# Hybrid attention and recurrence step: two gate chunks exchanged, modulation sums placed a chunk later, streams interleaved by other stage lengths

## Chip, cores and metric

One core of one Trainium2 chip. The metric is the device time of one execution in microseconds, smaller is better; the kernel before takes 966.97 us, the median of three runs (965.69 to 968.09).

## What is computed

Two layers (DEPTH = 2) over 640 tokens of 1,024 numbers: 512 latent tokens and 128 context tokens, all in float32. In each layer the tokens are modulated, go through one wide input projection, feed three parallel head groups, and come back through one output projection, a gate and a layer norm.

```python
shift, scale, gate = modulation(cond, w_ada[l], b_ada[l])      # cond differs for latent and context
h = x * (1.0 + scale) + shift
parts = split(h @ w_in[l])
# A: grouped-query attention, 8 query heads on 2 key heads, rms-normed and rotated q, k
# B: differential attention, 4 heads, two softmax maps each: p0 - lam * p1, rms-normed
# C: gated linear recurrence, 4 heads, forward and backward, state (64 x 64) per head
y = concat(A * silu(a_g), B * silu(d_g), C * silu(r_g)) @ w_out[l]
x = layer_norm(ALPHA * x + gate * y)
```

Latent tokens attend to 128 cached tokens besides their own 512, and their recurrence starts from a cached state; context tokens see themselves alone, and their keys, values and final states are outputs too.

## The kernel before, in words

**Tiles.** All 640 tokens are kept at once: SBUF buffers of 128 x 640 ("gran", 49 of them), 8 for the modulated input's high part and 8 for its low part. Every projection is three products, high x high, high x low, low x high (lines 351 to 353 for chunks with tokens on the partitions, 372 to 374 for transposed ones). The input projection is cut into 14 chunks of 256 columns (CHUNKS): 0 is q and k of the first head pair of B, 1 its values, 2 the values of C, 3 and 4 the two *gate chunks of the first recurrence pair*: 3 holds that pair's query gate (SiLU) and forward decay, 4 its backward decay and output gate (SiLU). 5 to 13 are the rest. A chunk's weights are loaded by SP (line 241) into a pool of three, cast by ScalarE (261) and their remainder taken by VectorE (262).

**Two kinds of work.** The chunks form the background: `bg_stream` (in `layer`) goes through them in the order of ORDER[l], with modulation products between them where MODS[l] says so. The foreground is six streams written as generators: `prep_stream` (rotation, lines 423 to 426; high and low parts, lines 99 to 103; transposes, line 1079), `sp_stream` (first pass of scores: product 1001 or 1005, row maximum on VectorE 1008, exponential on ScalarE 1009; then per pair of items the corrections, `finish_m` 983 to 986, turned into query rows by 1017 and 1020; for context tokens 1033, 1036, 1040, 1045, 1047), `pv_stream` (second scores 1057 to 1060, exponential 1066, values 1124), `hgrn_stream` (the recurrence, lines 822 to 978; its levels are line 882), and two that norm and gate the results.

**What sets the order.** `drive` writes all streams' code out in one order: it keeps a clock of its own, takes the first stream of PRIO[l] that is due, and otherwise the background. Each `yield` of a stage says how much TensorE time it takes and how long until the stream's next stage is due; these pairs are the table COST[l]. So COST sets only the order in which code is written. A scheduler of the framework then lays the instructions out for each engine, from that order; every engine runs its own list strictly in order, and SP's list of transfers too. LOOK, SPA, KG, OUTQ and PB are further constants that don't change here.

**Modulation sums.** `mod_next` multiplies 256 columns of the modulation weights (line 280) and ScalarE copies the result (`ms`, line 283). The sums over it (`mod_out`: two transposes on TensorE, 292; a reduction and an addition on VectorE, 295 and 299) wait in a list until `flush` is called. `bg_stream` calls it at the PEND-th piece of the next chunk and at every chunk's end:

```python
for r in chunks[i]() if kind == "w" else mod_next(l if i >= 8 else l + 1, i):
    n += kind == "w"
    if n == PEND:
        flush()
    ...
flush() if kind == "w" else None
```

**SiLU and decay.** `silu_block` reads a product out of PSUM by ScalarE (384), runs two more ScalarE steps (385, 386) and multiplies with the product, still in PSUM, on VectorE (387). `decay_block` takes its product out of PSUM in one VectorE clamp (565) and does all else in SBUF. The chunks' products use two PSUM banks ("A"), so a product waits until the one before the last has left its bank; everything small shares three banks ("B").

Of the kernel before, what the change touches and what calls it, by code (L numbers as in the profile page):

```python
# [37 lines left out]
WB = 6  # L38
KK = 8
LOOK = (0, 1)  # L40
PEND = 2
SPA = (2, 3)
KG = 4
OUTQ = (3, 2, 0, 1)
PB = dict(A=2, B=3, O=1)
OTAG = "O"
CTAG = "B"
COST = (dict(mod=(0.43, 2.59), norm0=(0.0, 4.0), norm1=(0.4, 0.96), gmix=(0.28, 21.63), h_exp=(0.06, 2.01),
              h_diag=(2.13, 0.37), h_lvl=(0.0, 3.0), h_mm=(0.99, 0.0), h_kst=(0.0, 1.4), h_tr=(0.0, 0.0),
              h_u=(7.96, 1.11), h_out=(22.66, 1.86), s_max=(0.0, 1.59), s_tr=(0.0, 0.4), c_max=(0.44, 3.0),  # L50
              c_tr=(1.29, 0.0), d_rq=(0.0, 1.96), d_rk=(0.53, 1.34), d_spl=(0.77, 1.38), d_tr=(4.22, 0.0),
              d_ctx=(0.72, 1.8), pv_c=(0.0, 0.0), g_ss=(0.0, 1.28), g_rope=(0.0, 2.5), g_k=(0.0, 0.71),
              g_ctx=(0.0, 1.2), g_spl=(0.0, 0.87), g_tr=(1.22, 2.24), pv_c2=(4.13, 5.2), s_g=(0.49, 1.79),
              s_d=(0.38, 1.88), pv_e=(0.77, 0.7), pv_g=(1.3, 0.56), pv_d=(1.04, 0.21)),
        dict(mod=(1.04, 9.27), norm0=(0.36, 5.04), norm1=(0.0, 0.68), gmix=(0.28, 21.63), h_exp=(0.0, 1.81),
              h_diag=(1.81, 1.27), h_lvl=(0.0, 3.0), h_mm=(0.89, 0.0), h_kst=(0.0, 1.63), h_tr=(0.0, 0.0),
              h_u=(7.96, 1.11), h_out=(22.66, 1.86), s_max=(0.0, 1.59), s_tr=(0.0, 0.19), c_max=(0.36, 3.68),
              c_tr=(1.29, 0.0), d_rq=(0.0, 1.96), d_rk=(0.53, 1.34), d_spl=(0.72, 1.39), d_tr=(3.82, 0.0),
              d_ctx=(0.6, 1.8), pv_c=(0.0, 0.28), g_ss=(0.0, 1.28), g_rope=(1.04, 4.49), g_k=(0.0, 0.71),
              g_ctx=(0.0, 1.2), g_spl=(0.07, 0.35), g_tr=(1.22, 2.24), pv_c2=(4.13, 5.4), s_g=(0.43, 1.82),  # L60
              s_d=(0.37, 1.67), pv_e=(0.77, 0.97), pv_g=(1.3, 0.73), pv_d=(0.86, 1.01)))
PRIO = ((1, 0, 2, 3, 5, 4),
        (0, 5, 1, 2, 3, 4))
ORDER = ((0, 1, 3, 4, 2, 5, 6, 8, 7, 9, 10, 11, 12, 13),
         (0, 1, 3, 2, 4, 5, 7, 6, 8, 9, 10, 11, 12, 13))
MODS = ({1: (8,), 2: (9,), 3: (10,), 4: (11,), 5: (0,), 6: (1,), 7: (2,), 8: (3,), 9: (4,), 10: (5,), 12: (6,), 13: (7,)},
        {0: (8,), 3: (9,), 9: (10,), 10: (11,)})
# [7 lines left out]
def hybrid_kernel(ctx: ExitStack, tc: tile.TileContext, A, cst, outs):  # L75
# [425 lines left out]
    def layer(l, hT, first, defer):  # L501
        cost.update(COST[l])
        lam_init = LAM0[l]
# [199 lines left out]
        def bg_stream():  # L703
            for kind, i in steps(l):
                n = 0
# [4 lines that stand above are left out]
# [703 lines left out]
```

## Time and profile before

| what | value |
|---|---|
| device time, median of 3 runs | 966.97 us (965.69 to 968.09) |
| the profiled execution | 973.31 us, span of its instructions 971.5 us |
| TensorE (PE) busy | 911.6 us, 94% of the span |
| weight loads on TensorE (PEld) | 751.6 us, 77% |
| VectorE (DVE) busy | 596.6 us, 61% |
| ScalarE (ACT) busy | 583.7 us, 60% |
| GpSimd (POOL) busy | 78.6 us, 8% |
| granted TensorE clock, mean | 0.977 of full speed |
| DMA | 100.36 MB, 103 GB/s over the span |
| chain that ended last | PE 65%, DVE 10%, DMA 10%, ACT 10%, issue 3%, SP's queue 2% |

A busy share is an average over stages. Where TensorE is busy nearly all the time, the lines to look for are its idle times and what ended each of them, and the stretches in which its clock was not granted in full. Matmuls overlap, so their listed durations are longer than the distance from one start to the next.

### The profile page before, as it was taken

What the parts mean: (1) busy time and instruction counts of PE and PEld (TensorE: products, weight loads), DVE (VectorE), ACT (ScalarE), POOL (GpSimd) and SP (SyncE); (2) the same over time, 40 slices, a digit from 0 to 9 for tenths busy, and PEclk for the clock granted to TensorE, in tenths of its full rate; (3) what the DMA queues carried; (4) which work ended last, traced back from release to release, by engine and by line L of the source; (5) the groups of instructions that cost most, each with busy time, mean ns of one, the idle gap of its engine ahead of it and who ended that gap; (6) DMA issues with size and microseconds to landing.
All of it is one profiled execution on the core that took longest, in us unless ns stands there. A gap on an engine that the chain in (4) does not pass through costs nothing.

```text
span 971.5 us, 20546 instructions
## 1 busy us (share of the span) xinstructions
PE 911.6 (94%) x8197; PEld 751.6 (77%) x8197; DVE 596.6 (61%) x1344; ACT 583.7 (60%) x1309; POOL 78.6 (8%) x113
## 2 busy tenths in 40 slices
PE   6999899999999989999999999999989998999995
PEld 3698776887878748687989997878768875878895
DVE  2346555945868875343698455685585885543467
ACT  2334665567667768773265468656766785886311
POOL 1000000200000100110023000020000000110012
PEclk9999897999999999999999999999989999999998
DMA  9856520344442121225624453025124121212322
GB/s 295 282 152 167 153 74 27 105 121 119 125 117 55 44 75 44 58 79 179 175 81 132 134 144 106 2 62 125 50 76 111 50 74 31 72 42 71 128 98 98
DMA packets 103583, 100.36 MB, mean 103 GB/s; under 512 B 9416, under 2 KB 91840, under 8 KB 103488
## 3 DMA queue, kind: packets, MB, share of 16 engines
q1 hardware_dynamic: 103488, 99.05, 34.7%
q8 instruction: 65, 1.06, 0.5%
q14 instruction: 30, 0.25, 0.1%
HBM read 77.25 MB, written 6.31 MB: 86 GB/s over the span
## 4 chain that ended last, share of the span: by engine, by line
PE 65%; DVE 10%; DMA 10%; ACT 10%; issue 3%; SPq 2%; DVEq 0%; POOL 0%; ACTq 0%; POOLq 0%
PE pO L1124 8%; PE pA L351 8%; PE pA L353 8%; PE pA L352 7%; PE pS L1001 5%; PE pA L374 4%; PE pA L372 4%; PE pA L373 4%; DMA wraw<-in_w_in_dram 3%; DMA wa<-in_w_ada_dram 2%; PE pB L1060 2%; PE pB L1057 2%; PE pS L1005 2%; ACT pS L1009 2%; PE pB L280 2%
## 5 line engine op out<-in xcount | busy, mean ns | idle before, releaser
L1008 DVE TENSOR_REDUCE nmx<-pS 128x1 f32<-128x640 f32 x128 | 105.4, 823 | 120.2 <-PE pS L1001 71.4
L351 PE MATMUL pA<-wh,mh 128*128 128x256 f32 x600 | 171.3, 286 | 1.6 <-DVE gate_t L387 1.3
L353 PE MATMUL pA<-wh,ml 128*128 128x256 f32 x600 | 170.8, 285 | 0.2 <-DVE ml L535 0.2
L352 PE MATMUL pA<-wl,mh 128*128 128x256 f32 x600 | 170.0, 284 | 0.0
L261 ACT CAST wh<-wraw 128x512 fp32r<-128x512 f32 x144 | 86.4, 621 | 75.5 <-PE pA L353 28.5
L262 DVE TENSOR_TENSOR wl<-wraw,wh 128x512 fp32r<-128x512 f32 x144 | 96.5, 695 | 53.1 <-ACT wh L261 50.0
L1009 ACT ACTIVATE pS<-pS,nmx 128x640 f32<-128x640 f32 x128 | 98.2, 767 | 50.4 <-DVE nmx L1008 48.2
L351 PEld LDWEIGHTS pA<-wh,mh 128*128 128x128 f32 x600 | 114.9, 191 | 4.2 <-DVE gate_t L387 1.6
L353 PEld LDWEIGHTS pA<-wh,ml 128*128 128x128 f32 x600 | 114.7, 191 | 1.6 <-issue 0.7
L352 PEld LDWEIGHTS pA<-wl,mh 128*128 128x128 f32 x600 | 114.7, 191 | 0.8 <-issue 0.6
L1066 ACT ACTIVATE PT<-pB 128x512 f32<-128x512 f32 x160 | 89.9, 599 | 28.8 <-PE pB L1060 15.6
L351 PE MATMUL pA<-wh,hh 128*128 128x256 f32 x240 | 71.4, 298 | 1.3 <-DVE gate_t L387 1.3
L372 PE MATMUL pA<-hh,wh 128*128 128x320 f32 x224 | 70.8, 316 | 0.0
L353 PE MATMUL pA<-wh,hl 128*128 128x256 f32 x240 | 70.7, 295 | 0.0
L352 PE MATMUL pA<-wl,hh 128*128 128x256 f32 x240 | 70.2, 293 | 0.0
L372 PE MATMUL pA<-mh,wh 128*128 128x320 f32 x224 | 70.2, 313 | 0.0
L374 PE MATMUL pA<-mh,wl 128*128 128x320 f32 x224 | 69.9, 312 | 0.0
L374 PE MATMUL pA<-hh,wl 128*128 128x320 f32 x224 | 69.7, 311 | 0.0
L373 PE MATMUL pA<-ml,wh 128*128 128x320 f32 x224 | 69.6, 311 | 0.0
L373 PE MATMUL pA<-hl,wh 128*128 128x320 f32 x224 | 69.5, 310 | 0.0
L1124 PE MATMUL pO<-PT,tk 128*64 128x512 f32 x256 | 67.0, 631 | 0.2 <-ACT PT L1066 0.2
L351 PEld LDWEIGHTS pA<-wh,hh 128*128 128x128 f32 x240 | 48.0, 200 | 3.8 <-DVE gate_t L387 1.6
(285 smaller groups left out, 1944.1 us busy)
## 6 DMA issues: line engine op xcount, KB each, us to landing
wraw<-in_w_in_dram SPq DMA_DIRECT2D x32, 512.0 KB
wraw<-in_w_ada_dram SPq DMA_DIRECT2D x32, 512.0 KB
wraw<-in_w_in_dram SPq DMA_DIRECT2D x48, 256.0 KB
wa<-in_w_ada_dram SPq DMA_DIRECT2D x32, 256.0 KB
wraw<-in_w_out_dram SPq DMA_DIRECT2D x16, 512.0 KB
Q<-Q SPq DMA_DIRECT2D x32, 160.0 KB
KD<-dkh SPq DMA_DIRECT2D x32, 96.0 KB
QD<-dqh SPq DMA_DIRECT2D x32, 80.0 KB
```

Of the source, the lines that this page charges most:

```text
L261: nc.scalar.copy(hi[n], src)
L262: tt(out=lo[n], in0=src, in1=hi[n].bitcast(F32), op=ALU.subtract)
L351: mm(out=ps[:, o:o + 256], lhsT=hi[k][:, sl], rhs=a, start=(n == 0), stop=False)
L352: mm(out=ps[:, o:o + 256], lhsT=hi[k][:, sl], rhs=b, start=False, stop=False)
L353: mm(out=ps[:, o:o + 256], lhsT=lo[k][:, sl], rhs=a, start=False, stop=(n == last))
L372: mm(out=ps, lhsT=wa, rhs=hi[k][:, sl], start=(k == 0), stop=False)
L373: mm(out=ps, lhsT=wa, rhs=lo[k][:, sl], start=False, stop=False)
L374: mm(out=ps, lhsT=wb, rhs=hi[k][:, sl], start=False, stop=(k == KB - 1))
L1008: dve.tensor_reduce(out=nmx[:, t, i:i + 1], in_=sv, axis=AX.XY, op=ALU.max, negate=True)
L1009: act(sv, sv, AF.Exp, bias=nmx[:, t, i:i + 1], accum_out=den[:, t, i:i + 1])
L1066: return pt, act(pt, ps, AF.Exp).ins
L1124: x = mm(out=o[64 * (i % 2):64 * (i % 2) + 64], lhsT=value(k, i % 2), rhs=pt, start=k == 0, stop=k == 4)
```

## The change

Four things, all of them constants that set the order in which the same instructions stand: ORDER[0] takes chunk 4 before chunk 3; PEND goes from 2 to 0, so that the list of modulation sums is no longer emptied inside a chunk but at its end; and both tables of COST get other values for some stages. PRIO has the same values on one line, so every line behind it is one lower in the changed file (262 becomes 261, and so on). The diff, without the unchanged lines of COST:

```diff
-PEND = 2
+PEND = 0
...
-COST = (dict(mod=(0.43, 2.59), norm0=(0.0, 4.0), norm1=(0.4, 0.96), gmix=(0.28, 21.63), h_exp=(0.06, 2.01),
+COST = (dict(mod=(0.43, 2.59), norm0=(0.0, 4.0), norm1=(0.4, 0.96), gmix=(0.35, 21.63), h_exp=(0.06, 2.01),
...
-              h_u=(7.96, 1.11), h_out=(22.66, 1.86), s_max=(0.0, 1.59), s_tr=(0.0, 0.4), c_max=(0.44, 3.0),
-              c_tr=(1.29, 0.0), d_rq=(0.0, 1.96), d_rk=(0.53, 1.34), d_spl=(0.77, 1.38), d_tr=(4.22, 0.0),
-              d_ctx=(0.72, 1.8), pv_c=(0.0, 0.0), g_ss=(0.0, 1.28), g_rope=(0.0, 2.5), g_k=(0.0, 0.71),
+              h_u=(7.96, 1.11), h_out=(22.66, 1.86), s_max=(0.0, 1.59), s_tr=(0.0, 0.2), c_max=(0.44, 3.0),
+              c_tr=(1.29, 0.0), d_rq=(0.0, 1.96), d_rk=(0.53, 1.34), d_spl=(0.77, 1.91), d_tr=(4.22, 0.0),
+              d_ctx=(0.72, 1.8), pv_c=(0.3, 0.3), g_ss=(0.0, 1.28), g_rope=(0.0, 2.5), g_k=(0.0, 0.71),
...
-        dict(mod=(1.04, 9.27), norm0=(0.36, 5.04), norm1=(0.0, 0.68), gmix=(0.28, 21.63), h_exp=(0.0, 1.81),
-              h_diag=(1.81, 1.27), h_lvl=(0.0, 3.0), h_mm=(0.89, 0.0), h_kst=(0.0, 1.63), h_tr=(0.0, 0.0),
-              h_u=(7.96, 1.11), h_out=(22.66, 1.86), s_max=(0.0, 1.59), s_tr=(0.0, 0.19), c_max=(0.36, 3.68),
-              c_tr=(1.29, 0.0), d_rq=(0.0, 1.96), d_rk=(0.53, 1.34), d_spl=(0.72, 1.39), d_tr=(3.82, 0.0),
+        dict(mod=(1.04, 9.27), norm0=(0.36, 5.34), norm1=(0.0, 0.68), gmix=(0.15, 21.63), h_exp=(0.0, 1.75),
+              h_diag=(1.09, 1.27), h_lvl=(0.0, 3.0), h_mm=(0.89, 0.0), h_kst=(0.0, 1.63), h_tr=(0.0, 0.0),
+              h_u=(7.96, 1.11), h_out=(22.66, 2.33), s_max=(0.3, 1.59), s_tr=(0.0, 0.19), c_max=(0.36, 3.68),
+              c_tr=(1.29, 0.0), d_rq=(0.0, 1.96), d_rk=(0.53, 1.34), d_spl=(0.72, 1.39), d_tr=(2.29, 0.0),
...
-              g_ctx=(0.0, 1.2), g_spl=(0.07, 0.35), g_tr=(1.22, 2.24), pv_c2=(4.13, 5.4), s_g=(0.43, 1.82),
-              s_d=(0.37, 1.67), pv_e=(0.77, 0.97), pv_g=(1.3, 0.73), pv_d=(0.86, 1.01)))
+              g_ctx=(0.0, 1.2), g_spl=(0.07, 0.35), g_tr=(1.22, 2.24), pv_c2=(4.13, 5.4), s_g=(0.34, 2.27),
+              s_d=(0.37, 1.67), pv_e=(0.77, 0.97), pv_g=(1.3, 0.44), pv_d=(0.86, 1.01)))
...
-ORDER = ((0, 1, 3, 4, 2, 5, 6, 8, 7, 9, 10, 11, 12, 13),
+ORDER = ((0, 1, 4, 3, 2, 5, 6, 8, 7, 9, 10, 11, 12, 13),
```

What this does to the engines' lists, at three places. The names: tk is a token chunk's result (here keys or queries being rotated), he the decay, gate_t a SiLU's result, sm and mod the modulation sums, dql and dkl low halves of queries and keys, wl the low half of a weight, mhl and mhc the corrections of scores (latent, context), QD and KD query and key rows of B, PT exponentials, dcv cached values.

**Place 1**, VectorE, first gate chunk of layer 0, the kernel before:

```order
L295 TENSOR_REDUCE sm<-pB 128x4
L299 SCALAR_TENSOR_TENSOR mod_105<-sm,vv 128x4
L387 TENSOR_TENSOR gate_t<-pA,sge 128x320
L423 TENSOR_TENSOR rope<-tk,cs 128x16x8 x4
L425 TENSOR_TENSOR tk<-tk,cs 128x512
L103 SCALAR_TENSOR_TENSOR dql<-pB,dqh 128x512
L262 TENSOR_TENSOR wl<-wraw,wh 128x512 x2
L426 TENSOR_TENSOR tk<-tk,rope 128x512
L387 TENSOR_TENSOR gate_t<-pA,sge 128x320
L100 TENSOR_TENSOR dkl<-pB,dkh 128x512
L100 TENSOR_TENSOR dkl<-pB,dkh 128x256
L103 SCALAR_TENSOR_TENSOR dql<-pB,dqh 128x128
```

VectorE in the change, the same place:

```order
L564 TENSOR_SCALAR he<-pA 128x320
L422 TENSOR_TENSOR rope<-tk,cs 128x16x8 x4
L424 TENSOR_TENSOR tk<-tk,cs 128x512
L425 TENSOR_TENSOR tk<-tk,rope 128x512
L102 SCALAR_TENSOR_TENSOR dql<-pB,dqh 128x512
L99 TENSOR_TENSOR dkl<-pB,dkh 128x512
L261 TENSOR_TENSOR wl<-wraw,wh 128x512 x2
L99 TENSOR_TENSOR dkl<-pB,dkh 128x256
L564 TENSOR_SCALAR he<-pA 128x320
L102 SCALAR_TENSOR_TENSOR dql<-pB,dqh 128x128
```

The modulation sums are gone from here, the clamp he stands where the SiLU's multiply stood, and the last rotation step (426, now 425) stands ahead of the weight's wl and not behind it.

**Place 2**, ScalarE at the end of a chunk that ends in a SiLU, with the copy ms of a modulation product (in the kernel before the second gate chunk, followed by the token chunk of C's values):

```order
L574 ACTIVATE hs<-hs,lbs 128x640
L283 COPY ms<-pB 128x256
L384 ACTIVATE sge<-pA 128x320
L1009 ACTIVATE pS,den<-pS,nmx 128x2x320
L385 ACTIVATE sge<-sge,cc 128x320
L386 ACTIVATE sge<-sge 128x320
```

ScalarE in the change (the first gate chunk, followed by the second):

```order
L573 ACTIVATE hs<-hs,lbs 128x640
L383 ACTIVATE sge<-pA 128x320
L282 COPY ms<-pB 128x256
L384 ACTIVATE sge<-sge,cc 128x320
L385 ACTIVATE sge<-sge 128x320
```

The copy ms has moved from ahead of the SiLU's first step to between the first and the second, and no score exponential (1009, now 1008) stands between.

**Place 3**, TensorE in layer 1, fourth pair of score passes, where its second scores begin, the kernel before:

```order
L1060 MATMUL pB<-QD,KD 128x512
L374 MATMUL pA<-mh,wl 128x320
L372 MATMUL pA<-mh,wh 128x320
L1060 MATMUL pB<-QD,KD 128x512 x2
L373 MATMUL pA<-ml,wh 128x320
L374 MATMUL pA<-mh,wl 128x320
L1060 MATMUL pB<-QD,KD 128x512
L1124 MATMUL pO<-PT,dcv 64x512 x2
L1124 MATMUL pO<-PT,tk 64x512 x2
L1045 MATMUL pB<-identr,mhc 8x128
L1060 MATMUL pB<-QD,KD 128x512 x2
```

TensorE in the change, from the last chunk products ahead of the fourth second score on:

```order
L371 MATMUL pA<-mh,wh 128x320
L372 MATMUL pA<-ml,wh 128x320
L373 MATMUL pA<-mh,wl 128x320
L1059 MATMUL pB<-QD,KD 128x512
L1044 MATMUL pB<-identr,mhc 8x128
L1059 MATMUL pB<-QD,KD 128x512
L1123 MATMUL pO<-PT,dcv 64x512 x2
L1123 MATMUL pO<-PT,tk 64x512 x2
L1059 MATMUL pB<-QD,KD 128x512
```

Ahead of the fourth second score (1060, now 1059) there are 27 chunk products in a row where there were two, and the context's correction (1045, now 1044) stands before the value products and not behind them.

VectorE there, up to the correction mhc that this transpose reads, the kernel before:

```order
L1036 TENSOR_REDUCE nmxc<-pS 128x4
L1175 TENSOR_TENSOR tk<-tk,gains 128x128
L577 SCALAR_TENSOR_TENSOR hg<-cs,hs 128x640
L423 TENSOR_TENSOR rope<-tk,gst 128x8x16 x4
L425 TENSOR_TENSOR tk<-tk,gct 128x512
L426 TENSOR_TENSOR tk<-tk,rope 128x512
L565 TENSOR_SCALAR he<-pA 128x320
L984 TENSOR_TENSOR nmxc<-nmxc,denc 128x4
L565 TENSOR_SCALAR he<-pA 128x320
L985 CAST mhc<-nmxc 128x4
L986 TENSOR_TENSOR mhc<-nmxc,mhc 128x4
```

VectorE in the change:

```order
L424 TENSOR_TENSOR tk<-tk,gct 128x512
L261 TENSOR_TENSOR wl<-wraw,wh 128x512
L425 TENSOR_TENSOR tk<-tk,rope 128x512
L571 SCALAR_TENSOR_TENSOR he<-he,lbs,hs 128x640
L261 TENSOR_TENSOR wl<-wraw,wh 128x512
L572 TENSOR_SCALAR hs<-hs,lbs 128x640
L983 TENSOR_TENSOR nmxc<-nmxc,denc 128x4
L1171 TENSOR_TENSOR tk<-tk,ss 128x640
L984 CAST mhc<-nmxc 128x4
L1174 TENSOR_TENSOR tk<-tk,gains 128x128
L576 SCALAR_TENSOR_TENSOR hg<-cs,hs 128x640
L985 TENSOR_TENSOR mhc<-nmxc,mhc 128x4
```

In both, the reduction nmxc of the context's maxima (1036, now 1035) comes first of the chain; in the change it is three rows above the first row shown, and a second norm and rotation of queries (1171, 1174) stand within the chain.

## Rows read from the trace of the kernel before

**Rows 1.** Windows, start-up to tail: TensorE, weight loads, VectorE, ScalarE, GpSimd, clock, DMA.

```profile
52.00:961.00 909.00, 870.04 (x7953) 725.75 (x7952) 571.56 (x1277) 565.22 (x1272) 75.55 (x105) 0.98 0.32 93
```

**Rows 2.** Windows at lower granted clock (columns as above), and the sum of all six.

```profile
108.56:115.38 6.82, 6.14 (x28) 6.15 (x29) 1.84 (x4) 3.85 (x9) 0.00 (x0) 0.50 0.70 175
...
722.96:729.78 6.82, 5.35 (x14) 2.32 (x15) 4.00 (x13) 3.14 (x9) 0.00 (x0) 0.50 0.00 0
815.12:818.53 3.41, 3.11 (x8) 0.77 (x8) 0.49 (x1) 2.23 (x5) 0.30 (x1) 0.50 0.38 95
sum 34.11, PE 30.87 PEld 20.62 DVE 14.61 ACT 20.70 POOL 0.30; mean PE 5.14 PEld 3.44 DVE 2.44 ACT 3.45 POOL 0.05
```

**Rows 3.** Waits of TensorE: who waited for whom, total us, times, longest us.

```profile
PE pS L1001 <- ACT pS L1009: 4.0, 9, 0.7
...
PE pB L292 <- ACT ms L283: 1.0, 2, 0.5
PE pB L1060 <- ACT QD L1020: 0.8, 1, 0.8
```

**Rows 4.** Timeline, VectorE and TensorE: start, us, engine, instruction, [idle before].

```profile
73.46 0.89 DVE L423 TENSOR_TENSOR rope<-tk,cs 128x128 f32<-128x128 f32 x4
...
77.38 1.29 DVE L262 TENSOR_TENSOR wl<-wraw,wh 128x512 fp32r<-128x512 f32 x2 [1.70 <-ACT wh L261]
78.59 0.69 DVE L426 TENSOR_TENSOR tk<-tk,rope 128x512 f32<-128x512 f32 x1
...
79.33 0.87 PE L1079 MATMUL pB<-cs,tk 128*128 128x128 f32 x6 [1.84 <-DVE tk L426]
...
82.11 0.48 DVE L565 TENSOR_SCALAR he<-pA 128x320 f32<-128x320 f32 x1
```

**Rows 5.** Timeline, layer 1, fourth score pair: TensorE and VectorE.

```profile
714.39 0.31 PE L372 MATMUL pA<-mh,wh 128*128 128x320 f32 x1
...
714.53 0.31 PE L373 MATMUL pA<-ml,wh 128*128 128x320 f32 x1
...
718.08 0.17 DVE L986 TENSOR_TENSOR mhl<-nmx,mhl 128x8 fp32r<-128x8 f32 x1
...
721.92 0.49 PE L1060 MATMUL pB<-QD,KD 100*128 100x512 f32 x1 [0.78 <-ACT PT L1066]
...
724.43 1.12 PE L1124 MATMUL pO<-PT,dcv 128*64 128x512 f32 x2 [2.02 <-ACT PT L1066]
...
725.78 0.16 DVE L986 TENSOR_TENSOR mhc<-nmxc,mhc 128x4 fp32r<-128x4 f32 x1
```

**Rows 6.** Timeline, end of layer 0's second gate chunk: ScalarE, TensorE, VectorE.

```profile
105.82 0.37 ACT L283 COPY ms<-pB 128x256 f32<-128x256 f32 x1 [0.33 <-PE pB L280]
...
107.36 0.56 PE L1001 MATMUL pS<-KD,QD 96*128 96x320 f32 x2 [0.68 <-ACT pS L1009]
...
108.70 0.48 DVE L387 TENSOR_TENSOR gate_t<-pA,sge 128x320 f32<-128x320 f32 x1
...
109.23 0.58 PE L351 MATMUL pA<-wh,hh 128*128 128x256 f32 x1 [1.31 <-DVE gate_t L387]
```

**Rows 7.** Timeline, TensorE, layer 1, first score pairs.

```profile
617.84 0.41 PE L1017 MATMUL pB<-identr,mhl 128*4 128x128 f32 x4 [0.68 <-DVE mhl L986]
...
624.91 0.22 PE L1045 MATMUL pB<-identr,mhc 128*8 128x128 f32 x1 [0.60 <-DVE mhc L986]
```

**Rows 8.** Timeline, TensorE, layer 0, sixth score pair and second recurrence pair.

```profile
341.24 0.40 PE L1017 MATMUL pB<-identr,mhl 128*4 128x128 f32 x4 [1.53 <-DVE mhl L986]
...
348.86 0.43 PE L977 MATMUL pB<-Ei,S 64*64 64x128 f32 x4 [1.07 <-DVE S L958]
```

**Rows 9.** Timeline, TensorE, layer 1, sixth score pair and second recurrence pair.

```profile
801.14 0.63 PE L939 MATMUL pB<-cs,kst 128*128 128x128 f32 x4 [0.81 <-DVE ss L413]
...
806.08 0.22 PE L1045 MATMUL pB<-identr,mhc 128*8 128x128 f32 x1 [0.95 <-DVE mhc L986]
...
815.42 1.12 PE L1124 MATMUL pO<-PT,avc 128*64 128x512 f32 x2 [0.76 <-ACT PT L1066]
```

More of the change, by code (lines that the diff above doesn't have):

```diff
@@ L59 @@
               d_ctx=(0.6, 1.8), pv_c=(0.0, 0.28), g_ss=(0.0, 1.28), g_rope=(1.04, 4.49), g_k=(0.0, 0.71),
-              g_ctx=(0.0, 1.2), g_spl=(0.07, 0.35), g_tr=(1.22, 2.24), pv_c2=(4.13, 5.4), s_g=(0.43, 1.82),
-              s_d=(0.37, 1.67), pv_e=(0.77, 0.97), pv_g=(1.3, 0.73), pv_d=(0.86, 1.01)))
-PRIO = ((1, 0, 2, 3, 5, 4),
-        (0, 5, 1, 2, 3, 4))
-ORDER = ((0, 1, 3, 4, 2, 5, 6, 8, 7, 9, 10, 11, 12, 13),
+              g_ctx=(0.0, 1.2), g_spl=(0.07, 0.35), g_tr=(1.22, 2.24), pv_c2=(4.13, 5.4), s_g=(0.34, 2.27),
@@ L65 @@
+              s_d=(0.37, 1.67), pv_e=(0.77, 0.97), pv_g=(1.3, 0.44), pv_d=(0.86, 1.01)))
+PRIO = ((1, 0, 2, 3, 5, 4), (0, 5, 1, 2, 3, 4))
+ORDER = ((0, 1, 4, 3, 2, 5, 6, 8, 7, 9, 10, 11, 12, 13),
          (0, 1, 3, 2, 4, 5, 7, 6, 8, 9, 10, 11, 12, 13))
```

## The prediction

> **What bounds the kernel now.** I read the page first and then one long stretch of it: after the start-up, from 52 to 961 us, TensorE is busy 870.04 of 909.00 us, and VectorE and ScalarE 571.56 and 565.22 [rows 1]. TensorE is the bound, and the change gives it the same matmuls, so only two things can move the time: the 39 us in which it waits inside that stretch, and the time at which it runs at half its clock. The table of windows shows the second: six stretches with a granted clock of 0.50 (the lower of the two levels, 1.2 of 2.4 GHz), 34.11 us in all [rows 2]; a stretch in which TensorE has work loses half its length, so up to 17 us. The list of waits, of which I use three rows [rows 3], says what TensorE waits for: after the start-up mostly a short chain through VectorE or ScalarE that the order of work does not cover. The timeline at the dearest of these waits is what I cost below.
>
> The profiled execution took 973.31 us, 6.34 above the median of 966.97; the sum is made against it and its difference taken off the median.
>
> **The change, part by part.**
>
> *Gate chunks exchanged, first pair of layer 0.* Now TensorE stands 1.84 us before the transposes of the rotated keys: VectorE's last rotation step at 78.59 is queued behind a weight split at 77.38 that waits for a transfer [rows 4]. In the new order that step stands ahead of the weight split, and of the low half of the queries (first pair of order rows). From the first finished product on, VectorE does one clamp (0.48), four quarter-rotations (0.89) and two steps of 0.69 each, 2.75 us; TensorE has 16 chunk products at 0.145 [rows 5] and five transposes to do meanwhile, some 2.9 us. So the wait goes: -1.8, bounds -1.84 and -0.9.
>
> The swap also takes the SiLU away from the place where it holds a PSUM bank ahead of a token chunk. There TensorE waits 0.68 and 1.31 us and, before that, 0.5 for the copy of the modulation sums [rows 3, 6]: ScalarE copies the sums at 105.82, then runs a SiLU, and VectorE's multiply at 108.70 frees the bank. The chunk that now ends there only clamps. But the same sequence arises 18 us earlier: the other gate chunk now ends in SiLU, and the second pair of order rows shows the copy of the sums between the first and second step of that SiLU. Without a score pass in between I price it at 2.0 (bounds 1.3, the multiply's wait alone, and 2.5, the whole): -2.5 + 2.0 = -0.5. The half-clock stretch that begins at 108.56 inside this wait [rows 2] I let move along: 0, bounds -3.4 and 0.
>
> *Modulation sums a chunk later.* Of the two waits on that copy, 1.0 us together [rows 3], the one in layer 1 has a whole chunk in front of it now: -0.5. The other is counted above. The sums are read only at the end of a layer, so lateness costs nothing there; the cover for that is the rest of the layer. The gate's store (line 318) moves back on SP's queue past a half of an input weight and two halves of a modulation weight; those no longer wait for it, and nobody reads the store before the layer's end, so I cost both at nothing. Between them the queue's transfers of key and query rows change places with weight loads by one or two; TensorE has no wait for a weight after 52 us among those costed here, and this too stands at nothing.
>
> *Streams interleaved anew.* Layer 1, first pairs: 0.68 before the transposes of the score corrections and 0.60 before those of the context [rows 7]; by the order they get 3.7 instead of 2.2 us of work in front, and 8.1 instead of 3.9. -1.3, bounds -1.3 and 0.
>
> Layer 1, fourth score pair: TensorE waits 0.78 and 2.02 us for ScalarE's exponentials [rows 5]. In the change 27 chunk products (3.9 us at 0.145) stand between the third and the fourth score tile, so these 2.8 us go. But the context's correction (line 1044 of the change) now comes ahead of the value products, 6.1 us after the score correction (34 chunk products, 4.9 us, and five others). What it waits for stands on VectorE: between the two corrections' last steps there were 17 instructions and 7.70 us (718.08 to 725.78, [rows 5]), and there are 23 now. At the same 0.45 each that is 10.4 us, a wait of 4.3. I take 4.0, bounds 0 and 4.9: +1.2 for the place. Behind this transpose on TensorE stand the fourth score tile and the value products, and nothing passes it.
>
> Layer 0, sixth score pair: the waits of 1.53 and 1.07 [rows 8] get 0.9 us more of chunk work each. -1.6 (0.7 of the first, since VectorE's queue there is as long as before), bounds -2.6 and 0.
>
> Layer 1, sixth pair: 0.81, 0.95 and 0.76 [rows 9] go, each with more work in front (21 products instead of 6; 11.2 us instead of 4.7; 2.7 instead of none): -2.5. New there: the score correction stands behind 29 VectorE instructions, 13 us at 0.45, with 10.6 us on TensorE. +2.0, bounds 0 and 2.5. The stretch at 815.12 begins just before the 0.76 wait ends and goes with it: -1.7, half of 3.41 [rows 2].
>
> Where score rows are turned into query rows, two pairs of layer 0 fall to 0.5 us of work between the transposes and the first tile; the one wait of this kind measured 0.8 [rows 3]. +0.9, bounds 0 and 1.6. Neighbouring score passes closer than 2.2 us go from 20 to 27 in layer 0 and from 23 to 20 in layer 1; they cost 4.0 us in nine waits now [rows 3]. 0, bounds -1 and +2.
>
> The sum: -1.8 -0.5 -0.5 -1.3 +1.2 -1.6 -0.5 +0.9 = -4.1, and -1.7 of clock: -5.8. 973.31 gives 967.5, and the median 966.97 gives **961.2 us**.
>
> On the clock, the rows show that the stretches at 108.56 and 722.96 begin inside waits of 1.31 and 2.02 [rows 2, 5, 6]; I therefore tie each to its wait. The Trainium skill, "TensorE: Matmul & The Clock Gate", in "A second HAM failure mode: psum-queue depth-cycling", describes a kernel whose clock swings because the array idles briefly and often between groups of matmuls, with no one long wait to blame. By that rule none of the 34 us would go with a single wait, and the sum would be 962.9.
>
> **The rivals.**
>
> *Slower: VectorE's queue in front of the corrections' transposes in layer 1.* The mechanism of +4.0 and +2.0 above, at its upper ends (4.9 and 2.5), with the tiles at theirs (1.6), and behind each of the two waits a half-clock stretch as at 722.96 (6.82, so 3.4 each), the one at 815.12 staying: -4.1 +0.9 +0.5 +0.7 + 6.8 = +4.8, **971.8**. It decides once these two waits and the clock lost behind them pass 14.7 us: the other terms with the clock of 815.12 save 11.8, and 2.9 is 0.3%, about what a measurement of this kernel can tell from no change. For it: 23 instructions against 17, counted in the order. Against it: the chain may start earlier, since TensorE runs ahead there.
>
> *No change: the profile's waits are not the timed runs'.* The timed runs lack 6.34 us of the profiled one. If what they lack is the stretch at 722.96 or that at 815.12 and the waits in front of them, then the change takes away what is mostly not there: 0 to -2, **966**. For it: the 6.34 is about these two stretches' loss, 5.1, and a wait. Against it: the waits rest on the order, which is the same in every run.
>
> *Faster by more: the new waits do not arise.* Weight splits in VectorE's queue are ready on time and its chain keeps pace: the +4.0, +2.0 and +0.9 fall away, and the stretch at 722.96 goes too (3.4): -5.8 -6.9 -3.4 = -16.1, **950.9**. For it: the order places each transpose by estimates of the same chains. Against it: so it did before, and 39 us of waits were left.
>
> **How the numbers follow.** Forecast 0.44 (956 to 964), more 0.17, no change 0.19, slower 0.20. Faster by over 0.3% (2.9 us): 0.44 + 0.17 = 0.61; within: 0.19; slower: 0.20. All lower bounds together give 945, all upper ones 976; for 8 in 10 I cut both ends by a few microseconds: 949 to 973. The forecast's own range is 956 to 964.
>
> **What would show it.** Right: no wait over 0.3 us at the turned keys near 79 us; about 2 us of waits where the first gate chunk of the change ends (near 87 us), and none after the second; value products of layer 1's fourth pair that do not wait, and a wait of 3 to 5 us at line 1044 just before them; a wait near 2 us at the sixth pair's line 1016. Wrong: that line 1044 does not wait at all (then it is nearer 951), or that half-clock time in the whole run is not below 34 us by about 3. The sum of the terms fails if the idle time from 52 to 961 us falls by more than 10 us or rises.

## The result, and the profile after

The changed kernel takes **954.74 us** in the median of 4 runs (950.55 to 957.86), beside 967.53 for the kernel before on the same chip: a ratio of 0.986, 95% interval 0.981 to 0.991. Six more runs of it, taken with the experiments, have a median of 955.89 and a ratio of 0.9875 (0.985 to 0.990). So the change saves 12 to 13 us. 961.2 was forecast, with a range of 949 to 973: the direction and the range hold, and the saving is twice the 5.8 us of the forecast.

The profiled execution took 957.86 us (span 956.1). Here is its stretch from the start-up to the tail, which answers to [rows 1], and its stretches at half clock, which answer to [rows 2] (columns as there: length; PE, PEld, DVE, ACT, POOL busy and counts; clock; DMA share; GB/s):

```profile
52.00:946.00 894.00, 860.32 (x7954) 720.95 (x7952) 572.04 (x1276) 563.29 (x1273) 76.75 (x105) 0.99 0.32 94
...
89.90:93.31 3.41, 3.26 (x12) 3.26 (x13) 0.59 (x2) 0.56 (x2) 0.00 (x0) 0.50 0.94 312
591.66:595.07 3.41, 3.41 (x10) 1.01 (x10) 1.22 (x2) 3.05 (x7) 0.00 (x0) 0.50 0.05 14
711.13:717.95 6.82, 6.19 (x16) 2.26 (x17) 5.25 (x14) 2.32 (x5) 0.00 (x0) 0.50 0.14 51
789.63:793.05 3.42, 3.42 (x15) 3.42 (x14) 3.42 (x9) 1.04 (x2) 0.00 (x0) 0.50 0.00 0
sum 17.06, PE 16.28 PEld 9.95 DVE 10.47 ACT 6.97 POOL 0.00; mean PE 4.07 PEld 2.49 DVE 2.62 ACT 1.74 POOL 0.00
```

The stretch is 15.0 us shorter than the 909.0 before, and TensorE's share of that falls into two parts. It waits 33.7 us instead of 39.0: 5.3 less. It is also *busy* 9.7 us less, with the same matmuls: 860.32 after 870.04. The second part is the larger one, and the prediction had only 1.7 us of it. Some of it is the clock: 17.06 us at half clock in place of 34.11. In those stretches TensorE was busy 16.28 us, and 30.87 before, and half of that is lost, so 15.4 becomes 8.1, which saves 7.3. The other 2.4 us lie neither in waits nor in the clock. (All of this compares one profile with one profile; what the timed runs say of the clock stands with the experiments.)

TensorE's largest waits (who waited for whom, total us, times, longest us), beside [rows 3]:

```profile
PE pB L1044 <- DVE mhc L985: 3.7, 3, 1.6
PE pB L291 <- ACT ms L282: 3.4, 1, 3.4
...
PE pB L938 <- DVE kst L931: 2.4, 1, 2.4
PE pB L1057 <- ACT Q L1019: 2.4, 4, 0.8
PE pS L1000 <- ACT pS L1008: 2.3, 6, 0.8
PE pB L1059 <- ACT PT L1065: 1.9, 1, 1.9
```

(A line here is one less than in the kernel before.) The wait at the turned keys has left the list, and score passes wait 2.3 instead of 4.0. New at the top are one wait of 3.4 for the copy of the modulation sums and one of 2.4 for the decayed keys of the second recurrence pair.

### The profile page after: what moved, and what is told of

The parts are those of the page before. It is cut to its first block, busy times and chain, and to the rows that moved or that the text cites. A ratio compares the mean times of both kernels' runs of the same rounds, so it can differ in the third digit from the quotient of the medians.

```text
span 956.1 us, 20537 instructions
## 1 busy us (share of the span) xinstructions
PE 902.5 (94%) x8197; PEld 747.6 (78%) x8197; DVE 597.7 (63%) x1344; ACT 581.7 (61%) x1309; POOL 79.7 (8%) x113
## 4 chain that ended last, share of the span: by engine, by line
PE 70%; DVE 12%; ACT 7%; DMA 7%; issue 2%; SPq 1%; POOL 0%; DVEq 0%; ACTq 0%; POOLq 0%
PE pO L1123 8%; PE pA L350 8%; PE pA L352 8%; PE pA L351 7%; PE pA L371 5%; PE pS L1000 5%; PE pA L372 5%; PE pA L373 5%; DMA wraw<-in_w_in_dram 4%; PE pB L1059 2%; PE pS L1004 2%; PE pB L1056 2%; PE pB L1057 2%; PE pB L279 2%; ACT pS L1008 1%
## 5 line engine op out<-in xcount | busy, mean ns | idle before, releaser
L350 PE MATMUL pA<-wh,hh 128*128 128x256 f32 x240 | 69.1, 288 | 0.0
L352 PE MATMUL pA<-wh,hl 128*128 128x256 f32 x240 | 68.4, 285 | 0.0
L351 PE MATMUL pA<-wl,hh 128*128 128x256 f32 x240 | 68.1, 284 | 0.0
L350 PEld LDWEIGHTS pA<-wh,hh 128*128 128x128 f32 x240 | 45.8, 191 | 2.8 <-issue 1.0
```

The lines of the kernel that those rows point to most:

```text
L350: mm(out=ps[:, o:o + 256], lhsT=hi[k][:, sl], rhs=a, start=(n == 0), stop=False)
L351: mm(out=ps[:, o:o + 256], lhsT=hi[k][:, sl], rhs=b, start=False, stop=False)
L352: mm(out=ps[:, o:o + 256], lhsT=lo[k][:, sl], rhs=a, start=False, stop=(n == last))
```

## The experiments

Theories at the start: (1) waits and half-clock stretches belong to places in the order, so each part of the change brings what its places show; (2) the half-clock stretches come and go by chance, and the 17 us are not the change's.

**The kernel before, profiled again** (no edit).

> The kernel before, unchanged, profiled a second time. Its first profile had 34.1 us at half clock between 52 and 961 us in six stretches (near 108, 149, 436, 603, 723 and 815 us) and 39 us of TensorE waits. Theory 'places' (each half-clock stretch belongs to a wait that the order makes): the same six places again, 31 to 37 us, time 965 to 972. Rival 'chance' (whether a wait is followed by half clock differs from one execution to the next): the waits are the same to 1 us, but stretches come at other places or are fewer, 15 to 28 us in all, and the time is shorter by half the difference. If the rival holds, the 17 us that the changed kernel's profile lacks at half clock are not the change's.

It ran at 966.67 us (ratio 0.9996, 0.997 to 1.002). Its profile, same two views:

```profile
52.00:955.00 903.00, 866.00 (x7952) 723.52 (x7951) 571.72 (x1275) 563.95 (x1271) 75.46 (x105) 0.99 0.32 93
...
108.98:112.39 3.41, 3.41 (x18) 3.41 (x17) 1.20 (x2) 1.59 (x5) 0.00 (x0) 0.50 0.63 138
146.53:156.77 10.24, 9.32 (x154) 8.84 (x155) 5.07 (x17) 6.09 (x17) 0.00 (x0) 0.50 0.16 54
433.20:436.60 3.40, 3.40 (x11) 1.06 (x9) 2.68 (x7) 1.99 (x5) 0.00 (x0) 0.51 0.00 0
720.00:723.40 3.40, 3.40 (x12) 1.59 (x9) 1.64 (x7) 1.51 (x3) 0.00 (x0) 0.50 0.00 0
808.70:812.10 3.40, 3.01 (x8) 0.77 (x8) 0.49 (x1) 2.32 (x5) 0.20 (x1) 0.50 0.39 99
```

Five of the six places come again; the one near 603 does not, and two are half as long: 23.9 us instead of 34.1. By the ranges set beforehand the 23.9 us are the second theory's (15 to 28), and five places out of six the first one's. So both are partly right: the places are the order's, whether and for how long the clock falls there differs from run to run. The first profile was one with much of it: by the working above (30.87 and 22.54 us busy at half clock) the difference is worth 4.2 us, which is most of why it lay 6.34 us above the median.

**The parts alone.** First the exchange, then the exchange with PEND = 0, then the two tables of stage lengths, each put into the kernel before.

```
e7_order    ORDER[0]: 0, 1, 3, 4, 2, ...  ->  0, 1, 4, 3, 2, ...
e1_front    the same, and PEND = 2 -> 0
e2_cost0    COST[0] of the change: gmix, s_tr, d_spl, pv_c
e3_cost1    COST[1] of the change: norm0, gmix, h_exp, h_diag, h_out, s_max, d_tr, s_g, pv_g
```

> The kernel before with the exchanged gate chunks and PEND = 0 alone, all stage lengths as before. From the two traces: the turned keys' 1.84 us go, the two waits at the end of a gate chunk are 4.9 in place of 2.5 (ScalarE waits 3.73 there for a weight), the half-clock stretch there is 3.4 in place of 6.8. Theory 'waits and clock add by place': -1.8 +2.4 -1.7 and -0.5 in layer 1 = -1.6, so 965 to 967. Rival 'the exchange carries the gain' (everything after it in layer 0 moves, and the stretches at 149 and 436 go with it): -7 to -9, so 958 to 961.

> The kernel before with the changed stage lengths of layer 0 alone. In the traces layer 0 is 11.1 us shorter after the change: 3.7 us of waits and 17.1 us less at half clock (8.5 us). Theory 'stage lengths of layer 0 end the stretches at 149 and 436': -6 to -9 (waits -2 to -3, clock -5 to -7), so 958 to 962, with under 10 us at half clock in layer 0. Rival 'the stretches belong to chance or to the exchange': -1 to -3, so 964 to 967, with 15 us or more at half clock in layer 0.

> The kernel before with the changed stage lengths of layer 1 alone. In the traces layer 1 with the tail is 4.3 us shorter after the change: about 2 us of waits, and some 2 us in which TensorE is busy for longer at the same 13.7 us of half clock. Theory 'the parts add by layer': -3 to -5, so 962 to 965, the waits at lines 1044 and 1059 of the fourth pair as after the change (2.5 us together) and one of 2.4 us at line 938. Rival 'what layer 1 gains comes from the state in which layer 0 leaves it': 0 to -1.5.

> The kernel before with the exchanged gate chunks alone, PEND as before. The front part with PEND = 0 gave -4.5 us (-3.7 in waits). The prediction put the exchange at -1.8 (turned keys) and -0.5 (gate chunk's end), the sums a chunk later at -0.5. Theory 'the exchange is what gains': -3 to -5, 963 to 965. Rival 'the sums' place gains' (two waits of 0.5 for their copy, and what they push): -1 or less, 966 to 968.

Then all but layer 1's lengths, that is the changed kernel with `COST[1]` of before:

> The changed kernel with the stage lengths of layer 1 as before: exchange, PEND = 0 and layer 0's lengths stay. Alone, the front part gave -4.5, layer 0's lengths -6.8, layer 1's 0 (waits -2.4 by the runs' times less half of their half-clock time, clock +2.1). Theory 'the parts add': -11 to -12 against the kernel before, 956 to 957, and the changed kernel's further 1 to 2 us are the waits of layer 1. Rival 'layer 1's lengths gain only behind the other two parts' (-2 or more): 958 to 960.

And the changed kernel itself once more:

> The changed kernel, unchanged, timed in more runs and profiled a second time. Four runs gave 954.74 with 28.6 us at half clock in a run (from each run's mean granted clock), where 29 runs of the kernel before had 35.2. Theory 'half of the waits' gain, a third of clock': median 953.5 to 955.5, half-clock time 26 to 31 us in the mean, the waits of the first profile again at lines 291, 1059 and 938 (3.4, 1.9, 2.4 us), and the 1.60 us at line 1044 near 424. Rival 'the four runs were lucky in their clock': 956 to 959 and 33 us or more at half clock.

| kernel | median, us | against before (95%) | layer 0, us | idle in it | at half clock in it | layer 1 and tail, us | at half clock in a run (runs) |
|---|---|---|---|---|---|---|---|
| before, first profile | 966.97 | | 416.4 | 21.3 | 20.5 | 450.5 | 34.8 (74) |
| before, again | 966.67 | 0.9996 (0.997 to 1.002) | 413.0 | 19.0 | 17.1 | 447.8 | 33.4 (10) |
| exchange alone | 965.62 | 0.998 (0.996 to 1.000) | 411.8 | 17.5 | 20.5 | 446.8 | 35.4 (12) |
| exchange, PEND = 0 | 963.23 | 0.995 (0.993 to 0.998) | 405.6 | 15.0 | 10.2 | 448.9 | 34.6 (12) |
| layer 0's lengths | 960.63 | 0.993 (0.990 to 0.996) | 408.1 | 16.2 | 13.7 | 445.4 | 28.5 (6) |
| layer 1's lengths | 967.22 | 0.9996 (0.998 to 1.001) | 414.7 | 20.9 | 17.1 | 447.6 | 39.4 (12) |
| all but layer 1's lengths | 956.41 | 0.988 (0.985 to 0.991) | 402.2 | 14.8 | 3.4 | 448.6 | 24.2 (6) |
| the change, first profile | 954.74 | 0.986 (0.981 to 0.991) | 405.3 | 17.6 | 3.4 | 446.2 | 28.6 (4) |
| the change, again | 955.89 | 0.9875 (0.985 to 0.990) | 403.8 | 15.6 | 6.8 | 444.6 | 30.8 (6) |

Layer 0 is counted from TensorE's first transposes of turned keys to its first transposes at the layer's end (line 333 of before), layer 1 from the end of those transposes on; idle time is TensorE's, summed over all its rows. These columns are each from one profile. The last column is from every timed run of the kernel (the first row's from all 74 of the kernel before): twice what the run's mean granted clock lacks to 1, times its span, in the mean. It takes in start-up and tail; single runs of one kernel scatter by 2 to 6 us around it.

Against the ranges set beforehand: exchange with PEND = 0 fell between its two, and so did the exchange alone; layer 0's lengths met the time (958 to 962), but not the under 10 us at half clock in layer 0; layer 1's lengths alone gave what the rival said; the kernel without them met its theory; and the change's second median lies between its two ranges, with the half-clock time of its theory.

The saving is layer 0's. The exchange with PEND = 0 brings 4.5 us and layer 0's lengths 6.8, and the kernel with both has the sum, 11.3. (The 2.1 of the exchange alone and the 2.4 that PEND = 0 adds are too near to each other's intervals to be told apart.) Layer 1's lengths bring nothing alone, and 0.5 to 1.7 on top of the rest, which no interval here separates from nothing. The kernels without layer 1's lengths span 445.4 to 450.5 us in layer 1: that is how far chance alone moves it.

Two things make up the 10 us of layer 0 in the profiles. TensorE's idle time there falls by 1.4 to 5.7, as a comparison of single profiles has it. And the half clock falls from 17 to 20 us, in all four profiles that have neither PEND = 0 nor layer 0's lengths, to 10 and 14 with the one or the other, and to 3.4, 3.4 and 6.8 with both.

The timed runs (last column) say how much of that is luck of a profile. The exchange with PEND = 0 has 34.6 us at half clock in the mean of its runs, as much as the kernel before: its 10 us in layer 0 were one profile's, and little of its 4.5 us can be clock. Layer 0's lengths do lower it, to 28.5, and to 24.2 with the other two parts. Layer 1's lengths raise it again: alone to 39.4, and on top of the rest from 24.2 to 28.6 and 30.8, which costs up to 2 to 3 us and is one reason why they bring so little. Half of the difference being lost, the clock is worth up to 5.3 us of the 11.3, and up to 2.5 of the change's 12 to 13. The second theory, chance alone, has no reason for that; it falls, though the places alone do not settle a stretch either (below).

**The late weight half.** At the end of the first gate chunk of the changed kernel (timelines of ScalarE, TensorE and SP's queue; start, us, engine, instruction, [idle before]):

```profile
85.66 1.14 ACT L260 CAST wh<-wraw 128x512 fp32r<-128x512 f32 x2 [3.73 <-DMA wraw<-in_w_in_dram]
86.70 0.82 ACT L573 ACTIVATE hs<-hs,lbs 128x640 f32<-128x640 f32 x1
87.43 0.41 ACT L383 ACTIVATE sge<-pA 128x320 f32<-128x320 f32 x1
87.75 0.36 ACT L282 COPY ms<-pB 128x256 f32<-128x256 f32 x1
```

```profile
83.65 1.07 PE L279 MATMUL pB<-wraw,sc 128*32 128x256 f32 x16
88.16 0.44 PE L291 MATMUL pB<-cs,ms 128*128 128x128 f32 x2 [3.44 <-ACT ms L282]
90.05 0.63 PE L371 MATMUL pA<-hh,wh 128*128 128x320 f32 x1 [1.45 <-DVE gate_t L386]
```

```profile
78.28 0.62 SPq L94 DMA_DIRECT2D KD<-dkh x1
79.07 1.07 SPq L240 DMA_DIRECT2D wraw<-in_w_in_dram x2
80.19 0.53 SPq L94 DMA_DIRECT2D KD<-dkh x1
```

The views name the copy (L282) and the SiLU's product (L386). But the copy, the SiLU and a decay step all stand behind a weight cast, and ScalarE stands still 3.73 us until that weight lands. Its transfer was issued on SP's queue at 79.07, when a raw buffer came free, among those of key and query rows, which the earlier turned keys now send from 78.28 to 84.15. In the kernel before the like transfer was issued at 78.70, the first key row followed at 80.80, and the cast at 82.74 did not wait for it. That the rows are what slows it was not tried by itself; that it is late, and what follows, two edits to the changed kernel test:

```
e4_raw4   GRAN = 49 -> 48;  tag="raw", name="wraw", bufs=3 -> 4
e9_mods   MODS[0]: {1: 8, 2: 9, 3: 10, 4: 11, 5: 0, ...} -> {1: 8, 3: 9, 4: 10, 5: 11, 6: 0, ...}
```

> The changed kernel with four buffers for raw weight halves in place of three, and one granule fewer (48) to make room. In the changed kernel's trace TensorE waits 3.44 and 1.45 us near 85 us, where ScalarE had waited 3.73 us for a raw half whose transfer was issued at 79.07, when its buffer came free, beside the transfers of key rows; a half-clock stretch of 3.41 follows. Theory 'the late weight half holds up ScalarE's queue': with a buffer more the half is there in time, ScalarE's wait at that place is under 0.5, TensorE's 4.9 become 1.3 to 2: -3 to -5 with the clock, 950 to 952. Rival 'the wait is the SiLU's and the copy's own chain': 4 us or more stay there, and the time is within 1.5 us of the changed kernel.

> The changed kernel with layer 0's modulation products, from the second on, one place later in the list, so that the weights of the second gate chunk are loaded ahead of the modulation weight that follows the first. TensorE's order at that boundary still has a modulation product there. Theory 'the late weight half holds up ScalarE's queue': ScalarE does not wait 3.73 us there; TensorE waits 1 to 2.5 us in all, for the modulation weight or the SiLU, in place of 4.9: -2 to -4, 951 to 953, if the later places cost nothing. Rival 'SiLU and copy, not the weight': 4 us or more stay, 954 to 956.

With the fourth buffer the weight's cast there no longer waits, and 4.89 us of TensorE's waits become 2.63:

```profile
85.34 0.60 ACT L260 CAST wh<-wraw 128x512 fp32r<-128x512 f32 x1
85.85 0.43 ACT L383 ACTIVATE sge<-pA 128x320 f32<-128x320 f32 x1
...
88.28 0.41 PE L371 MATMUL pA<-hh,wh 128*128 128x320 f32 x1 [2.63 <-DVE gate_t L386]
```

953.29 us in the median of 6 runs, ratio 0.984 (0.981 to 0.987): the lowest of all kernels here, 2.1 below the 955.4 of the change's ten runs, though the intervals overlap, and short of the 950 to 952 expected. What is left there is the SiLU's own chain behind a decay step and a cast. With the modulation weight loaded later the 4.89 fall to 0.23, and yet the kernel takes 959.57, 4.2 above the change where 2 to 4 below were expected: TensorE waits 2.18 us at the turned keys again, 1.81 near 145, with half-clock stretches at both, and its runs have 34.1 us at half clock in the mean. The second gate chunk's weight now stands ahead: ScalarE waits 4.31 us for it before its cast at 73.35, and VectorE's split of it at 74.00 stands ahead of the clamp and the rotation, where in the change it stands behind them, at 77.50. So the late weight is the cause at that place, and both prices were too high: the next chain was late in its turn.

**The decayed keys of layer 1.** In the changed kernel VectorE's last steps of the rotation stand between the two that make the decayed keys, and TensorE waits 2.40 us (VectorE, then TensorE):

```profile
786.14 0.68 DVE L425 TENSOR_TENSOR tk<-tk,rope 128x512 f32<-128x512 f32 x1
...
787.47 0.82 DVE L931 TENSOR_TENSOR kst<-he,kst 128x640 f32<-128x640 f32 x1
...
788.35 0.66 PE L938 MATMUL pB<-cs,kst 128*128 128x128 f32 x4 [2.40 <-DVE kst L931]
```

```
COST[1]:  h_kst=(0.0, 1.63) -> (0.0, 3.0)      e12: with four raw buffers; e13: with three
```

> The changed kernel with the fourth raw buffer and, in layer 1 alone, 3.0 in place of 1.63 as the length of the stage that makes the decayed keys (h_kst). TensorE's transposes of them (line 938, second recurrence pair) then stand behind the score and context corrections and 55 chunk products. In the run with the fourth buffer TensorE waits 3.55 us there for VectorE's last multiply, and a half-clock stretch of 3.41 follows. Theory 'VectorE's queue is long there and the transposes can go behind other work': that wait falls under 1, the corrections' waits stay under 1.5: -2.5 to -4.5 against 953.3, so 949 to 951. Rival 'another chain of the same queue is late next' (the corrections' own chain, now with nothing in front): 952 to 955.

> The same length of 3.0 for that stage in layer 1, on the changed kernel with its three raw buffers: TensorE's transposes stand directly behind the context correction there, with chunk products in front of both. Theory 'VectorE's queue': the 2.40 us at line 938 and the 0.94 at line 1016 become under 1.5 together, the stretch of 3.41 behind them goes: -2 to -4, 951 to 953. Rival 'another chain is late next': 954 to 956. Against the run with the fourth buffer and this length, the buffer's worth is 1.5 us if the two are independent.

955.24 and 954.62 us (0.986 and 0.986, each within 0.003): the rival holds, as far as the time goes. The wait at line 938 (2.40, and 3.55 in the run with four raw buffers) is gone in both, and a chunk product now waits for the SiLU instead, 2.48 us with four raw buffers and 1.31 with three:

```profile
784.01 0.41 PE L371 MATMUL pA<-mh,wh 128*128 128x320 f32 x1 [2.48 <-DVE gate_t L386]
```

That wait is not all: with this length TensorE also needs about 2 us more of busy time behind layer 0, which no list of waits has (next part).

**A seam in a product.** The 2.4 us outside waits and clock are not an accident of one profile: by the same working the kernel before needs 854.6 and 854.7 us of TensorE at full clock in its two profiles, the changed one 852.2 and 851.9. Of all lines the modulation products change most. TensorE in before, then in the changed kernel:

```profile
284.33 0.63 PE L280 MATMUL pB<-wraw,sc 128*32 128x256 f32 x4
284.89 0.66 PE L1154 MATMUL pO<-PT,tk 128*64 128x128 f32 x8
285.47 0.63 PE L280 MATMUL pB<-wraw,sc 128*32 128x256 f32 x6
286.04 0.56 PE L1001 MATMUL pS<-k,Q 128*128 128x320 f32 x2
286.43 0.46 PE L1005 MATMUL pS<-k,Q 72*128 72x320 f32 x2
286.82 0.63 PE L280 MATMUL pB<-wraw,sc 128*32 128x256 f32 x6
287.38 0.39 PE L351 MATMUL pA<-wh,hh 128*128 128x256 f32 x1
```

```profile
279.68 1.07 PE L279 MATMUL pB<-wraw,sc 128*32 128x256 f32 x16
280.68 0.39 PE L350 MATMUL pA<-wh,hh 128*128 128x256 f32 x1
```

In one piece the product takes 1.00 us from its first start to the next instruction's. In three pieces it takes 0.56, 0.57 and 0.56, 1.69. Before, 24 pieces make up the 16 products after 52 us; in the change 19. To price a seam by itself, one was put into every product (zr is a tile of zeros):

```
+            if h == 0:
+                mm(out=ps[:, 0:32], lhsT=zr, rhs=rw[0][:, 0, 0:32], start=False, stop=False)
```

> The changed kernel with one short matmul of zeros (all 128 columns of weights, 32 columns wide, added into the same sums) in the middle of each of the 16 modulation products after 52 us. In the traces a product in one piece takes 1.00 us of TensorE and one in two pieces 0.55 + 1.00, with whatever stands between counted apart; before has 8 products in two or three pieces, the changed kernel 3, and no view lists the difference as a wait. Theory 'a seam inside a product costs TensorE about 0.5 us without showing as a wait': a product grows from 1.0 to 1.5 or 1.6, +7 to +9 in all, 962 to 964 against 955 for the changed kernel. Rival 'the seam is free, what the pieces cost is other waiting': a product grows by the short matmul alone, under 0.15 each, +2 at most, 955 to 957.

963.30 us in 12 runs, ratio 0.995 (0.993 to 0.998): 7.9 above the change, as the theory has it. (Some 0.9 of that can be clock, 31.7 us at half clock in a run in place of 29.9.) A product now takes 1.48 in place of 1.00:

```profile
205.22 0.64 PE L282 MATMUL pB<-wraw,sc 128*32 128x256 f32 x8
205.79 0.41 PE L285 MATMUL pB<-wraw,zr 128*128 128x32 f32 x2
206.13 0.64 PE L282 MATMUL pB<-wraw,sc 128*32 128x256 f32 x8
```

The two zero matmuls start 0.14 apart; how the rest of the 0.48 divides between the second one and the two hand-overs, the rows do not tell. No view lists it as a wait. So putting one more seam into a product does cost what was said. Why a product in pieces costs more is less sure: a piece of 2, 4, 6 or 8 matmuls takes 0.55 to 0.57, one of 10 to 16 from 0.98 on, so that a cut after 2 leaves two pieces as long as a piece of 8 and a whole product. This experiment put its seam between two halves of 8 and does not tell the hand-over from such a step.

Nor do the seams account for the 2.4 us. Here is the stretch from the turned keys to the end of TensorE's work, cut at the layer's end (line 333), before and then changed:

```profile
73.26:489.64 416.38, 395.07 (x3653) 321.69 (x3650) 253.65 (x531) 261.64 (x581) 26.09 (x36) 0.98 0.36 102
489.64:961.10 471.46, 453.74 (x4129) 383.61 (x4129) 308.37 (x697) 296.82 (x672) 49.46 (x69) 0.99 0.28 83
```

```profile
73.17:478.47 405.30, 387.65 (x3655) 315.91 (x3653) 251.96 (x528) 261.52 (x584) 26.97 (x36) 1.00 0.36 105
478.47:946.00 467.53, 451.50 (x4129) 384.79 (x4129) 309.48 (x696) 296.40 (x672) 49.78 (x69) 0.99 0.29 83
```

Less half of what was busy at half clock (18.99 and 11.87 us before, 3.26 and 13.02 in the change), TensorE needs 385.6 and 447.8 us at full clock before, and 386.0 and 445.0 in the change. In layer 0 the figure is 384.8 to 386.0 in all profiles but the one with the added seams (389.3), however many pieces its products have. Behind it, it is 447.8 to 448.4 in the six with layer 1's lengths of before, and 444.5 to 445.1 in the five with the change's lengths and no added seam, that of layer 1's lengths alone among them; with h_kst = 3.0 it is 447.0 and 446.8, although with four raw buffers layer 1's products stand in one piece there. So the busy time that the change saves comes with layer 1's lengths. Two seams fewer in products make about 1.2 us of it; what makes the rest was not found. (In layer 0 three seams fewer save as much on the products, and the transposes of their sums take 1.1 more.)

## Why the prediction was right, and where not

**The waits.** Forecast -4.1, measured -5.3 between the first profiles and -4.3 between the second ones (36.6 us in 52 to 954.6, then 32.3 in 52 to 943.8). The sum is right, and by luck: by the terms below, the places that were costed change by about -0.8 together, where -4.1 were forecast. The rest of the 5.3 came from waits that had no price or 0, among them those of score passes (4.0 to 2.3), the 1.25 and 0.80 near 149 and the 1.50 near 895 (all three gone), while 1.23 near 121 and 1.49 near 261 are new. The terms:

- Turned keys, -1.8: right, no wait is left near 79.
- End of the first gate chunk, 2.5 to 2.0: wrong. The cluster did move there, and the second chunk ends without a wait, but it costs 4.89 and, in the second profile, 3.42. The step that failed is "without a score pass in between I price it at 2.0": ScalarE's queue there also holds a weight cast, and I had let transfers of key rows and weights change places "by one or two" at nothing. Here such a place counts. The half-clock stretch moved along, as said.
- Modulation sums in layer 1, -0.5: right. First pairs of layer 1, -1.3: the 0.68 and 0.60 went, but at line 1153 behind them 0.41 became 1.32.
- Fourth score pair of layer 1, +1.2: the queue was right and the wait wrong. Rows:

```profile
702.26 0.17 DVE L985 TENSOR_TENSOR mhl<-nmx,mhl 128x8 fp32r<-128x8 f32 x1
...
709.63 0.83 ACT L573 ACTIVATE hs<-hs,lbs 128x640 f32<-128x640 f32 x1 [0.88 <-DVE hs L572]
710.37 2.04 ACT L1065 ACTIVATE PT<-pB 128x512 f32<-128x512 f32 x4
...
711.00 0.70 PE L1059 MATMUL pB<-QD,KD 100*128 100x512 f32 x1 [1.92 <-ACT PT L1065]
712.05 0.14 DVE L985 TENSOR_TENSOR mhc<-nmxc,mhc 128x4 fp32r<-128x4 f32 x1
...
712.34 0.27 PE L1044 MATMUL pB<-identr,mhc 128*8 128x128 f32 x1 [0.63 <-DVE mhc L985]
```

  Between the two corrections' last steps VectorE takes 9.8 us; 10.4 were forecast. But the same queue holds up a decay step on ScalarE, the exponentials stand behind that, and so TensorE is stopped one instruction earlier, at line 1059, for 1.92; line 1044 then waits 0.63 and not 4.0. Together 2.55, where 2.80 were before. The value products do not wait, as said.
- Sixth pair of layer 0, -1.6: 1.53 and 1.07 became 0.35.
- Sixth pair of layer 1: the three waits went, and line 1016 waits 0.9 where 2.0 were forecast; but line 938 waits 2.40, of which nothing was said, and the half-clock stretch I took off with the 0.76 begins behind that wait now.
- Turned score rows into query rows, +0.9: the waits for line 1019 go from 2.2 to 3.4 and 4.3, but in layer 0, which was meant, to 1.7 and 2.6; the others are new, in layer 1 near 839 and 875.

**What carried the miss** is layer 0: -3.0 forecast, -11.3 measured without layer 1's lengths. The 3.0 were all waits. TensorE's idle time there falls by 4.2 to 6.5 (21.3 and 19.0 us become 14.8), its busy time at full clock stays the same, and the clock brings up to 5.3 us by the timed runs. The step that failed is the one that put layer 0's half-clock stretches at nothing: the one at 108.56 "I let move along: 0", and those near 149 and 436 had no term.

The first paragraph's step "only two things can move the time" fails as well. There are three: the busy time at full clock, which fell by 2.4 to 2.8 us and had no term. It came with layer 1's lengths, and where they stand alone the time does not fall, their runs having more half clock (39.4 us). The pieces of products are the one part of it that was found. The Trainium skill, "TensorEngine Tiling (Array Packing)", in "Key Properties", says that changing the tiling mode drains TensorE; the 0.48 us for a full matmul put into a product of 32 columns fit that, though they do not prove it.

**The clock**, forecast -1.7, measured -7.3 between the first profiles and -3.7 between the second. From the mean granted clock of all runs, half-clock time, with start-up and tail, is 34.8 us over 74 runs of before and 29.9 over ten of the change: which is worth at most 2.5 us: more than the 1.7, and far from the 7.3 of two profiles. What was mis-sized is the choice of which stretches go. I took off one in layer 1, which stayed at its new place, and gave none to the 10.24 us at 149 and the 3.41 at 436, since I had not costed the waits there; those are the ones that layer 0 lost in these profiles. Tying each stretch to its wait holds for one of the two: near 149 the waits of 1.25 and 0.80 went, and the stretch with them; near 436 the wait of 1.60 stayed and the stretch went all the same (last section). So the rule weighed in the prediction, that none would go with a single wait, is neither shown nor refuted here.

**Of the rivals**, "slower" failed at its condition: lines 1044 and 1016 cost 0.63 and 0.9 in layer 1, not 4.9 and 2.5, since their chains stopped TensorE elsewhere, and the stretch at 711 was there before. (At its own upper ends, 7.4 of waits and 6.8 of clock, it came to 14.2, short of the 14.7 that it named as its mark; the mark counts the stretch at 815 as gone, the rival lets it stay.) "No change" was right that the profile held more half clock than most runs, and wrong that the change acts on that alone. "Faster by more" is right in that the new waits did not arise as priced, but most of what it adds to the forecast was to come from layer 1 (4.0, 2.0 and a stretch of 3.4), and layer 1 gave 0 to 2. The split by layers is the plain error under a direction that held: -3.0 forecast for layer 0, -11.3 measured without layer 1's lengths; -2.8 for layer 1, -0.4 measured with them alone.

## What to carry to other kernels

Where one engine is busy 95% of the time, split its time into three, not two: waits, time at the lower clock, and the busy time that is left, which changes of order move too (2 to 3 us here; a cut in a product of another tiling, 0.3 to 0.6 us, shows in no list of waits). When a chain is made earlier, follow the transfers that it sends earlier, and whose they delay. And take a second profile of the kernel before ahead of costing single stretches of half clock: five of six places came again, but 34 us became 24. The mean granted clock of every timed run then says how much of the clock is the change's.

## What was not expected of the hardware

Every one of the 64 half-clock stretches between 60 and 935 us in the 14 profiles begins close behind a wait of TensorE, or several, of which the longest is 0.58 us or more. (Some begin before the wait ends.) But a wait need not bring one: counting a stretch that begins between the wait's start and 2.5 us past its end, 40 of the 56 waits of 1.5 us or more have one, 14 of 79 between 1.0 and 1.5, and 38 of 437 between 0.25 and 1.0. The same wait of 1.60 us before the context correction near 430 us stands in 12 profiles (in the two others, with four raw buffers, it is 1.45 and 1.47, without a stretch); in 8 the clock fell behind it, in 4 (both profiles of the change, the exchange alone, and the kernel without layer 1's lengths) it stayed at full. What decides it there stays open: none of these runs tells the four apart from the eight. A stretch of 3.4 costs up to 1.7 us, and the 10.2 us between the two profiles of before make 4.2 of the 6.4 by which their times differ (973.31 and 966.89).
